# One transpose for both key blocks' factors in a sliding-window attention, with the softmax's small steps done for four heads together

## The chip, the cores and the metric

The kernel runs on one core of a Trainium2 chip. The metric is device time in microseconds (us) from launch to end. Lower is better. A core has five engines that run side by side, each with an instruction queue of its own that it works through in order: TensorE (PE in the rows; its weight loads are listed as PEld), VectorE (DVE), ScalarE (ACT), GpSimd (POOL) and SyncE (SP, here only issuing transfers). Matrix products land in PSUM, everything else lives in SBUF.

## The reference, cut to what matters

Two decoder layers run for a prompt of 1024 tokens and for 8 sample tokens. Layer 0 mixes tokens with gated linear attention, layer 1 with sliding-window attention (window 128, 16 query heads in 4 groups, one learned sink per head), and each is followed by a squared-ReLU MLP. The change lies wholly in the prompt's window attention:

```python
def sink_probs(scores, mask, sinks):
    s = jnp.where(mask, scores, -jnp.inf)
    sk = sinks.astype(jnp.float32).reshape(SWA_KV_HEADS, SWA_GROUP)[:, :, None, None]
    m = jnp.maximum(jnp.max(s, axis=-1, keepdims=True), sk)
    p = jnp.exp(s - m)
    return p / (jnp.sum(p, axis=-1, keepdims=True) + jnp.exp(sk - m))

def swa_attend_prompt(q, k, v, sinks):
    ...
    kk, vv = with_prev(k), with_prev(v)      # keys of the block before, then of the own block
    scores = jnp.einsum('bnqkgd,bnskd->bnkgqs', qb, kk).astype(jnp.float32) * (SWA_HEAD_DIM ** -0.5)
    i = jnp.arange(SWA_BLOCK)[:, None]
    j = jnp.arange(2 * SWA_BLOCK)[None, :]
    diff = SWA_BLOCK + i - j
    mask = (diff >= 0) & (diff <= SWA_WINDOW) & (key_pos >= 0)
    p = sink_probs(scores, mask[None, :, None, None], sinks)
    o = jnp.einsum('bnkgqs,bnskd->bnqkgd', p.astype(vv.dtype), vv)
```

For a query at place i of its block of 128, the mask leaves the keys j >= i of the block before and the keys j <= i of its own block. The two triangles meet only on the diagonal.

## The kernel before

The prompt is cut into two groups of 512 tokens, A (which also carries the 8 sample tokens) and B. Every weight product is a job of `lin` (L280): weights are fetched, split on ScalarE and VectorE into a rounded part and a remainder (L204, L205), and three products per tile are summed (L224, L226, L228). These jobs are the foreground.

Everything else, the attention too, is a generator in a queue `bg`. After each job `tick` (L171) hands out credit, and the front generator runs on until its `yield`s have used the credit up; `need` (L180) runs a generator to its end before a job that depends on it. So A's attention is strewn over B's first MLP, and B's attention over A's second MLP. A scheduler then decides each engine's own order, so that on ScalarE and VectorE it is not simply the order of the text.

`swa_attention` (L943) works on 16 units per group, one for each of 4 key heads and 4 blocks of 128 queries; a unit holds 4 query heads, as 2 x 2 tiles (m and i). Its steps are:
- `queries` (L969): the unit's queries are split into rounded part and remainder, two casts on ScalarE (L976, L977) and two subtractions on VectorE (L978, L979).
- `softmax` (L981): twice (for m = 0, 1) four products give scores in PSUM (L990); VectorE adds the mask and takes the maximum (L996), does small steps on 128x2 numbers (L1000 to L1002, L1007, L1008), ScalarE takes exponentials (L1004, L1006), and VectorE scales the factors in place (L1010).
- `turn` (L1013): for each of the two key blocks, four 128x128 transposes on TensorE (L1019) into a PSUM tile `ppt`, then `split` (L297) into `ph` on ScalarE (L298) and `pl` on VectorE (L299).
- `values` (L1025): four products with the values (L1030, L1031), then a few copies and sums into the output.

The first unit of each key head in A has no block before it and only one key block; the other 28 of the 32 units have two. In step i of the loop (L1042) the text has `turn` of unit i-2 and `softmax` of unit i-1, then a `yield PACE`, then `values` of unit i-2 and `queries` of unit i, then a `yield PACE`. Each stretch between two yields is called a half-step below.

The factors stand in tiles of tag `pb`, 4 buffers (`PB`); the value job's `vT`, `ko` and `srow` take the same tag. GpSimd does little in these stretches: it issues some transfers, and in the rotary step of the jobs before, it multiplies (L879) while VectorE multiplies and adds (L880, L881).

Of the kernel before, what the change touches and what calls it, by code (L numbers as in the profile page):

```python
# [12 lines left out]
F32 = mybir.dt.float32  # L13
# [7 lines left out]
P = 128  # L21
# [14 lines left out]
PB = 4  # L36
# [32 lines left out]
def tile_hybrid_gla_swa_decoder(  # L69
# [779 lines left out]
    def swa_qkv(S, sp, g, box, needs):  # L849
# [41 lines left out]
        def vjob(m):  # L891
            cell = {}

            def pre_v():
                cell["v"] = sp.tile([P, NMAX], F32, tag="pb", name="vT", bufs=PB)

# [36 lines left out]
    def swa_cache_out(sp, g):  # L933
# [4 lines left out]
        ko = sp.tile([P, 256], F32, tag="pb", name="ko", bufs=PB)  # L938
# [4 lines left out]
    def swa_attention(S, sp, g):  # L943
# [25 lines left out]
        def queries(u):  # L969
# [8 lines left out]
            nc.vector.tensor_tensor(out=qs[dn, 0], in0=q[up], in1=r(qs[up, 0]), op=ALU.subtract)  # L978
            nc.vector.tensor_tensor(out=qs[up, 1], in0=q[dn], in1=r(qs[dn, 1]), op=ALU.subtract)  # L979

        def softmax(u):  # L981
            kh, kl = keys[u.j]
            k0, n = u.k0, u.n
            u.p = []
            for m in range(2):
# [6 lines left out]
                pb = sp.tile([P, 2, 256], F32, tag="pb", name="pb", bufs=PB)  # L992
                st = sp.tile([P, 8], F32, tag="st", name="st", bufs=4)
                mx = sp.tile([P, 2], F32, tag="mx", name="mx", bufs=4)
                for i in range(2):
                    nc.vector.tensor_tensor_reduce(out=pb[:, i, k0:], in0=ps[:, i, k0:], in1=S.mask[:, k0:],  # L996
                                                   scale=1.0, scalar=-3e38, op0=ALU.add, op1=ALU.max,
                                                   accum_out=mx[:, i:i + 1])
                sk = S.sink[:, 4 * u.j + 2 * m:4 * u.j + 2 * m + 2]
                nc.vector.tensor_tensor(out=mx, in0=mx, in1=sk, op=ALU.max)  # L1000
                nc.vector.tensor_tensor(out=st[:, 0:2], in0=sk, in1=mx, op=ALU.subtract)
                nc.vector.tensor_scalar_mul(mx, mx, -1.0)  # L1002
# [3 lines left out]
                nc.scalar.activation(out=st[:, 0:2], in_=st[:, 0:2], func=AF.Exp)  # L1006
                nc.vector.tensor_tensor(out=st[:, 4:6], in0=st[:, 0:2], in1=st[:, 2:4], op=ALU.add)  # L1007
                nc.vector.reciprocal(out=st[:, 4:6], in_=st[:, 4:6])  # L1008
# [438 lines left out]
```

## Time and profile before

| | us |
|---|---|
| median of 3 runs | 2279.63 |
| the runs | 2278.18 to 2283.04 |
| the profiled execution | 2278.29 |
| its span, first to last instruction | 2276.5 |
| TensorE busy in the span | 2248.2 |
| VectorE busy | 1477.4 |
| ScalarE busy | 1233.3 |
| GpSimd busy | 83.1 |
| granted clock of TensorE, mean share of full speed | 0.998 |

The profile follows one execution. Busy time of an engine is the union of its instructions; TensorE's instructions overlap, so an instruction's own duration is longer than the distance to the next one. "Releaser" is what ended a wait.

### The profile page before, as it was taken

The numbers are of one execution on the slowest core, as the hardware profiler recorded it, in microseconds if no ns is written. First come the engines' busy times: TensorE is split into PE (matmuls) and PEld (weight loads), VectorE is DVE, ScalarE is ACT, GpSimd is POOL, SyncE is SP. The second block draws the span as 40 slices with busy tenths as digits, with TensorE's granted clock in tenths as the row PEclk, the third lists the DMA queues.
The fourth block names the chain that finished last, engine by engine and source line by source line (L and its number), as shares of the span: only waits on it lengthen the run. The fifth ranks groups of instructions, "written<-read, shape, count | busy, mean of one in ns | idle before, by whom it ended". The sixth has DMA issues, their size and how long they took to land.

```text
span 2276.5 us, 39219 instructions
## 1 busy us (share of the span) xinstructions
PE 2248.2 (99%) x14600; PEld 2041.6 (90%) x14600; DVE 1477.4 (65%) x3203; ACT 1233.3 (54%) x2608; POOL 83.1 (4%) x123
## 2 busy tenths in 40 slices
PE   7999999999999999999999999999999999999998
PEld 7998889889999998998888989989999899888886
DVE  6587666676644457566887487758888478544445
ACT  6656644466434446545776456636767456443433
POOL 3010000100000000020000000010000000000000
PEclk9999999999999999999999999999999999999999
DMA  6443322345333335333222354433222354533322
GB/s 169 130 131 99 102 79 74 111 144 163 90 93 89 93 94 171 97 111 93 79 86 73 98 168 126 135 107 86 75 75 80 93 158 130 163 117 97 102 82 81
DMA packets 389216, 247.26 MB, mean 109 GB/s; under 512 B 17848, under 2 KB 368152, under 8 KB 388224
## 3 DMA queue, kind: packets, MB, share of 16 engines
q1 hardware_dynamic: 360768, 196.85, 30.1%
q10 hardware_dynamic: 24000, 25.58, 3.8%
q0 software_dynamic: 4256, 22.31, 3.0%
q8 instruction: 115, 1.88, 0.3%
q14 instruction: 77, 0.63, 0.1%
HBM read 221.19 MB, written 24.25 MB: 108 GB/s over the span
## 4 chain that ended last, share of the span: by engine, by line
PE 54%; DVE 1%; issue 0%; ACT 0%; DMA 0%; DVEq 0%; ACTq 0%
PE psl L224 14%; PE psl L228 14%; PE psl L226 14%; PE psd L1269 2%; PE psd L1271 2%; PE psd L1270 2%; PE psc L990 1%; PE ppt L1019 1%; PE po L1030 1%; PE po L1031 1%; DVE xtail L1313 0%; PE pfin L1178 0%; DVE yf L1298 0%; DMA kc<-in_cache_swa_k_dram 0%; PE pxt L1224 0%
## 5 line engine op out<-in xcount | busy, mean ns | idle before, releaser
L224 PE MATMUL psl<-xh,wh 128*128 128x512 f32 (+2 forms) x2784 | 891.0, 320 | 0.5 <-ACT sr L532 0.3
L228 PE MATMUL psl<-xh,wl 128*128 128x512 f32 (+2 forms) x2784 | 886.3, 319 | 1.1 <-DVE wl L205 0.9
L226 PE MATMUL psl<-xl,wh 128*128 128x512 f32 (+2 forms) x2784 | 886.2, 318 | 0.2
L204 ACT CAST wh<-wst 128x512 fp32r<-128x512 f32 x656 | 405.9, 620 | 596.4 <-PE psl L226 475.7
L205 DVE TENSOR_TENSOR wl<-wst,wh 128x512 fp32r<-128x512 f32 x656 | 457.9, 700 | 301.2 <-ACT wh L204 281.5
L228 PEld LDWEIGHTS psl<-xh,wl 128*128 128x128 f32 x2784 | 523.3, 188 | 38.8 <-DVE wl L205 1.6
L224 PEld LDWEIGHTS psl<-xh,wh 128*128 128x128 f32 x2784 | 524.3, 188 | 37.1 <-ACT sr L532 0.6
L226 PEld LDWEIGHTS psl<-xl,wh 128*128 128x128 f32 x2784 | 524.1, 188 | 36.7 <-DVE xl L299 0.9
L224 PE MATMUL psl<-hh,wh 128*128 128x256 f32 (+2 forms) x1280 | 390.8, 305 | 0.0
L226 PE MATMUL psl<-hl,wh 128*128 128x256 f32 (+2 forms) x1280 | 390.7, 305 | 0.0
L228 PE MATMUL psl<-hh,wl 128*128 128x256 f32 (+2 forms) x1280 | 390.3, 305 | 0.0
L224 PEld LDWEIGHTS psl<-hh,wh 128*128 128x128 f32 x1280 | 240.9, 188 | 11.2 <-ACT hh L298 0.5
L226 PEld LDWEIGHTS psl<-hl,wh 128*128 128x128 f32 x1280 | 240.7, 188 | 11.0
L228 PEld LDWEIGHTS psl<-hh,wl 128*128 128x128 f32 x1280 | 240.8, 188 | 10.7
L299 DVE TENSOR_TENSOR hl<-rl,hh 128x256 fp32r<-128x256 f32 (+1 forms) x192 | 98.7, 514 | 166.9 <-ACT hh L298 166.3
L814 DVE TENSOR_TENSOR yf<-yf,psl 128x256 f32<-128x256 f32 (+2 forms) x280 | 132.8, 474 | 82.8 <-PE psl L228 80.7
L801 ACT ACTIVATE rl<-psl 128x256 f32<-128x256 f32 (+1 forms) x192 | 87.3, 454 | 94.9 <-PE psl L228 83.5
L1269 PE MATMUL psd<-wls,hh 128*128 128x512 f32 x256 | 101.5, 397 | 0.0
L1271 PE MATMUL psd<-whs,hh 128*128 128x512 f32 x256 | 100.6, 394 | 0.0
L1270 PE MATMUL psd<-wls,hl 128*128 128x512 f32 x256 | 100.5, 393 | 0.0
L802 ACT ACTIVATE rl<-rl 128x256 f32<-128x256 f32 (+1 forms) x192 | 94.5, 492 | 4.5
L298 ACT CAST hh<-rl 128x256 fp32r<-128x256 f32 (+1 forms) x192 | 92.3, 481 | 4.7 <-ACT rl L802 0.7
(332 smaller groups left out, 2365.2 us busy)
## 6 DMA issues: line engine op xcount, KB each, us to landing
wst<-in_ffn_w_up_dram SPq DMA_DIRECT2D x256, 256.0 KB
wst<-in_ffn_w_down_dram SPq DMA_DIRECT2D x256, 256.0 KB
wst<-in_gla_w_in_dram SPq DMA_DIRECT2D x96, 256.0 KB
wst<-in_swa_w_qkv_dram SPq DMA_DIRECT2D x48, 256.0 KB
wst<-in_gla_w_out_dram SPq DMA_DIRECT2D x32, 256.0 KB
wst<-in_swa_w_out_dram SPq DMA_DIRECT2D x32, 256.0 KB
nx<-xs ACTq DMA_DIRECT2D x24, 260.0 KB
xs<-y POOLq DMA_DIRECT2D x2, 2080.0 KB, 8.1
```

What stands on the lines that cost most here:

```text
L204: nc.scalar.copy(out=wh[:, :, :m], in_=st[:, :, :m])
L205: nc.vector.tensor_tensor(out=wl[:, :, :m], in0=st[:, :, :m], in1=r(wh[:, :, :m]), op=ALU.subtract)
L224: nc.tensor.matmul(o, lhsT=wh[:, k % 4, :m], rhs=xh[:, k, c0:c0 + n], start=(k == 0), stop=False)
L226: nc.tensor.matmul(o, lhsT=wh[:, k % 4, :m], rhs=xl[:, k, c0:c0 + n], start=False, stop=False)
L228: nc.tensor.matmul(o, lhsT=wl[:, k % 4, :m], rhs=xh[:, k, c0:c0 + n], start=False, stop=(k == kt - 1))
L298: nc.scalar.copy(out=h, in_=src)
L299: nc.vector.tensor_tensor(out=l, in0=src, in1=r(h), op=ALU.subtract)
L802: nc.scalar.activation(out=rl, in_=rl, func=AF.Square)
L814: nc.vector.tensor_tensor(out=o, in0=o, in1=ps, op=ALU.add)
L1269: nc.tensor.matmul(ps, lhsT=h[:, tok], rhs=wh, start=(k == 0), stop=False)
L1270: nc.tensor.matmul(ps, lhsT=l[:, tok], rhs=wh, start=False, stop=False)
L1271: nc.tensor.matmul(ps, lhsT=h[:, tok], rhs=wl, start=False, stop=(k == HB - 1))
```

## The change

`turn` transposes once instead of twice. For units with two key blocks, GpSimd adds the unscaled factors of the block before (`a`) onto those of the own block (`b_`), and then keeps of `a` only its diagonal (a product with the identity). The scaling by the reciprocal sum moves from VectorE to ScalarE and follows these two. Four transposes bring the summed factors into one PSUM tile; a copy under the mask `late` (j > i) takes the upper triangle into `a`, whose diagonal is there already, and a subtraction leaves the rest in `b_`. Both are then split as before, now from SBUF.

The small softmax steps are done once on 128x4 numbers instead of twice on 128x2. The two subtractions in `queries` move from VectorE to GpSimd. The factors of a unit now share one tile (2 buffers of 128x1024 instead of 4 of 128x520). The loop is reordered: `softmax` of unit i-1 and `queries` of unit i, yield, `values` of unit i-3 and `turn` of unit i-2, yield; so the transposes come three half-steps behind the scores instead of two, and the value products two behind the transposes instead of one. There are 36 yields either way. `late` is made once, from `cmask`, when the layer is set up.

```diff
-PB = 4
+PB = 2
@@ swa_setup
+        S.late = sp.tile([P, P], F32, name="late")
+        nc.gpsimd.dma_start(out=S.late, in_=cmask)
+        nc.vector.tensor_scalar(out=S.late, in0=S.late, scalar1=-1.0, scalar2=1.0, op0=ALU.mult, op1=ALU.add)
@@ queries
-            nc.vector.tensor_tensor(out=qs[dn, 0], in0=q[up], in1=r(qs[up, 0]), op=ALU.subtract)
-            nc.vector.tensor_tensor(out=qs[up, 1], in0=q[dn], in1=r(qs[dn, 1]), op=ALU.subtract)
+            nc.gpsimd.tensor_tensor(out=qs[dn, 0], in0=q[up], in1=r(qs[up, 0]), op=ALU.subtract)
+            nc.gpsimd.tensor_tensor(out=qs[up, 1], in0=q[dn], in1=r(qs[dn, 1]), op=ALU.subtract)
@@ softmax
-            u.p = []
+            pb4 = sp.tile([P, D], F32, tag="pb", name="pb", bufs=PB).rearrange("p (i m k) -> p i m k", i=2, m=2)
+            u.p = pb4
+            st = sp.tile([P, 16], F32, tag="st", name="st", bufs=4)
+            mx = sp.tile([P, 4], F32, tag="mx", name="mx", bufs=4)
             for m in range(2):
                 ps = aux([P, 2, 256], "psc")
...
-                sk = S.sink[:, 4 * u.j + 2 * m:4 * u.j + 2 * m + 2]
...
+            sk = S.sink[:, 4 * u.j:4 * u.j + 4]
+            nc.vector.tensor_tensor(out=mx, in0=mx, in1=sk, op=ALU.max)
+            nc.vector.tensor_tensor(out=st[:, 0:4], in0=sk, in1=mx, op=ALU.subtract)
+            nc.vector.tensor_scalar_mul(mx, mx, -1.0)
+            for m in range(2):
                 for i in range(2):
-                    nc.scalar.activation(out=pb[:, i, k0:], in_=pb[:, i, k0:], func=AF.Exp, bias=mx[:, i:i + 1],
-                                         accum_out=st[:, 2 + i:3 + i])
...
+                    h = 2 * m + i
+                    nc.scalar.activation(out=pb4[:, i, m, k0:], in_=pb4[:, i, m, k0:], func=AF.Exp,
+                                         bias=mx[:, h:h + 1], accum_out=st[:, 4 + h:5 + h])
+            nc.scalar.activation(out=st[:, 0:4], in_=st[:, 0:4], func=AF.Exp)
+            nc.vector.tensor_tensor(out=st[:, 8:12], in0=st[:, 0:4], in1=st[:, 4:8], op=ALU.add)
+            nc.vector.reciprocal(out=st[:, 8:12], in_=st[:, 8:12])
+            if u.first:
+                scale(u, st)
+                return
+            a, b_ = (pb4[:, :, :, c:c + P] for c in (0, P))
+            nc.gpsimd.tensor_tensor(out=b_, in0=b_, in1=a, op=ALU.add)
+            nc.gpsimd.tensor_tensor(out=a, in0=a, in1=ident.unsqueeze(1).unsqueeze(1).to_broadcast([P, 2, 2, P]),
+                                    op=ALU.mult)
+            scale(u, st)
+
+        def scale(u, st):
+            for m in range(2):
                 for i in range(2):
-                    nc.vector.tensor_scalar_mul(pb[:, i, k0:], pb[:, i, k0:], st[:, 4 + i:5 + i])
+                    pb = u.p[:, i, m, u.k0:]
+                    nc.scalar.activation(out=pb, in_=pb, func=AF.Identity, scale=st[:, 8 + 2 * m + i:9 + 2 * m + i])
@@ turn
-            for kk in ((1,) if u.first else (0, 1)):
-                pt = aux([P, 2, 2, P], "ppt")
...
+            pt = aux([P, 2, 2, P], "ppt")
+            for i in range(2):
+                for m in range(2):
+                    nc.tensor.transpose(pt[:, i, m, :], u.p[:, i, m, P:], ident)
...
+            late = S.late.bitcast(mybir.dt.uint32).unsqueeze(1).unsqueeze(1).to_broadcast([P, 2, 2, P])
+            a, b_ = (u.p[:, :, :, c:c + P] for c in (0, P))
+            nc.vector.copy_predicated(out=a, mask=late, data=pt)
+            nc.vector.tensor_tensor(out=b_, in0=pt, in1=a, op=ALU.subtract)
+            for kk, t in enumerate((a, b_)):
+                split(*halves(kk), t)
@@ the loop
-        for i in range(nu + 2):
...
+        for i in range(nu + 3):
             if 1 <= i <= nu:
                 softmax(units[i - 1])
-            yield PACE
-            if i >= 2:
-                values(units[i - 2])
             if i < nu:
                 if units[i].n == 0:
                     prep_k(units[i].j)
                 queries(units[i])
-            yield PACE
+            if i > 0:
+                yield PACE
+            if i >= 3:
+                values(units[i - 3])
+            if 2 <= i < nu + 2:
+                if units[i - 2].n == 0:
+                    prep_v(units[i - 2].j)
+                turn(units[i - 2])
+            if i < nu + 2:
+                yield PACE
```

## Rows read from the trace of the kernel before

**Rows 1.** The page: busy engines, then the chain that ended last, by line.
```profile
PE 2248.2 (99%) x14600; PEld 2041.6 (90%) x14600; DVE 1477.4 (65%) x3203; ACT 1233.3 (54%) x2608; POOL 83.1 (4%) x123
PE psl L224 14%; PE psl L228 14%; PE psl L226 14%; PE psd L1269 2%; PE psd L1271 2%; PE psd L1270 2%; PE psc L990 1%; PE ppt L1019 1%; PE po L1030 1%; PE po L1031 1%; DVE xtail L1313 0%; PE pfin L1178 0%; DVE yf L1298 0%; DMA kc<-in_cache_swa_k_dram 0%; PE pxt L1224 0%
```
**Rows 2.** TensorE's waits in 1046:1246 (A) and 1550:1783 (B): total, times, longest.
```profile
PE ppt L1019 <- DVE pb L1010: 0.5, 1, 0.5
...
PE psc L990 <- DVE kl L958: 0.3, 1, 0.3
```
**Rows 3.** Busy us by stretch, A then B: PE, PEld, DVE, ACT, POOL; clock.
```profile
1080.00:1240.00 160.00, 159.54 (x794) 133.56 (x793) 136.64 (x451) 112.18 (x294) 3.65 (x6) 1.00 0.28 81
1575.00:1745.00 170.00, 170.00 (x1388) 167.89 (x1387) 145.23 (x476) 119.83 (x332) 1.12 (x2) 1.00 0.28 79
```
**Rows 4.** Chain in order of time (start, us), then timeline of weight loads.
```profile
1603.95 0.87 PE ppt L1019 x8
...
1210.67 0.59 PEld L1019 LDWEIGHTS ppt<-ident,pb 128*128 128x128 f32 x4
...
1223.47 1.02 PEld L1019 LDWEIGHTS ppt<-ident,pb 128*128 128x128 f32 x8
```
**Rows 5.** Line L1019: duration ns min/median/max, first and last start.
```profile
L1019 PE MATMUL ppt<-ident,pb x240: 270/272/328, 1058.5 to 1772.4; 128*128 128x128 f32 x120
```
**Rows 6.** VectorE's groups in 1575:1745 (count | busy us, mean ns | idle); last row: by line.
```profile
L205 DVE TENSOR_TENSOR wl<-wst,wh 128x512 fp32r<-128x512 f32 x48 | 32.9, 687 | 4.8 <-ACT wh L204 3.6
L299 DVE TENSOR_TENSOR pl<-ppt,ph 128x512 fp32r<-128x512 f32 x24 | 15.9, 685 | 0.5
L1010 DVE TENSOR_SCALAR pb<-pb,st 128x256 f32<-128x256 f32 x48 | 14.7, 348 | 0.5
L299 DVE TENSOR_TENSOR hl<-rl,hh 128x256 fp32r<-128x256 f32 (+1 forms) x25 | 10.6, 425 | 10.4 <-ACT hh L298 10.4
L979 DVE TENSOR_TENSOR qs<-q,qs 64x256 fp32r<-64x256 f32 x12 | 5.1, 421 | 0.4
L1007 DVE TENSOR_TENSOR st<-st 128x2 f32<-128x2 f32 x24 | 3.8, 157 | 1.7 <-ACT pb L1004 1.3
...
L656 DVE COPY_PREDICATED att_sb<-cm,patt x8: 729/745/756, 101.3 to 397.5; 128x512 f32<-128x512 uint32 x8
```
**Rows 7.** ScalarE's groups in the same stretch, then single instructions from the timeline.
```profile
L802 ACT ACTIVATE rl<-rl 128x264 f32<-128x264 f32 (+1 forms) x24 | 10.1, 422 | 0.4
...
1606.24 0.40 ACT L977 CAST qs<-q 64x256 fp32r<-64x256 f32 x1
...
1609.16 0.49 ACT L1004 ACTIVATE pb<-pb,mx 128x256 f32<-128x256 f32 x1
```
**Rows 8.** Timeline of GpSimd and VectorE where GpSimd multiplies (start, us, idle before).
```profile
1515.26 1.28 POOL L879 TENSOR_TENSOR qsw<-qsw,sin 128x512 f32<-128x512 f32 x1 [4.14 <-DMA qsw<-q]
1515.77 1.32 DVE L205 TENSOR_TENSOR wl<-wst,wh 128x512 fp32r<-128x512 f32 x1 [0.71 <-ACT wh L204]
...
1547.77 1.29 POOL L879 TENSOR_TENSOR qsw<-qsw,sin 128x512 f32<-128x512 f32 x1 [4.16 <-DMA qsw<-q]
1548.30 0.43 DVE L814 TENSOR_TENSOR yf<-yf,psl 128x264 f32<-128x264 f32 x1 [1.02 <-PE psl L228]
```
**Rows 9.** VectorE's idle time ahead of L881 (20 instructions): releaser, us, times.
```profile
  POOL qsw L879: 1.1, 2
```
**Rows 10.** Timelines of one unit's scores and scaling; then the shortest stretch in A.
```profile
1605.49 0.28 PE L990 MATMUL psc<-kl,qs 128*128 128x256 f32 x1
1611.26 0.62 DVE L1010 TENSOR_SCALAR pb<-pb,st 128x256 f32<-128x256 f32 x2
...
1155.13 0.39 PE L1030 MATMUL po<-ph,vv 128*128 128x512 f32 x1
...
1168.60 0.37 PEld L1019 LDWEIGHTS ppt<-ident,pb 128*128 128x128 f32 x2
1169.66 0.68 PEld L1019 LDWEIGHTS ppt<-ident,pb 128*128 128x128 f32 x6 [0.69 <-DVE pb L1010]
```

More of the change, by code (lines that the diff above doesn't have):

```diff
@@ L894, in pre_v @@
             def pre_v():
-                cell["v"] = sp.tile([P, NMAX], F32, tag="pb", name="vT", bufs=PB)
+                cell["v"] = sp.tile([P, D], F32, tag="pb", name="vT", bufs=PB)
             def ev(ps, c0, n):
@@ L937, in swa_cache_out @@
             nc.tensor.transpose(pt[:, m, :], g.kr[:, m, P + 384:P + 512], ident)
-        ko = sp.tile([P, 256], F32, tag="pb", name="ko", bufs=PB)
+        ko = sp.tile([P, D], F32, tag="pb", name="ko", bufs=PB)[:, :256]
         nc.vector.tensor_copy(out=ko, in_=pt.rearrange("p m d -> p (m d)"))
@@ L991, in softmax @@
                                          start=(kx is kh), stop=(kx is kl))
-                pb = sp.tile([P, 2, 256], F32, tag="pb", name="pb", bufs=PB)
-                st = sp.tile([P, 8], F32, tag="st", name="st", bufs=4)
-                mx = sp.tile([P, 2], F32, tag="mx", name="mx", bufs=4)
                 for i in range(2):
-                    nc.vector.tensor_tensor_reduce(out=pb[:, i, k0:], in0=ps[:, i, k0:], in1=S.mask[:, k0:],
+                    nc.vector.tensor_tensor_reduce(out=pb4[:, i, m, k0:], in0=ps[:, i, k0:], in1=S.mask[:, k0:],
@@ L1006, in softmax @@
-                nc.scalar.activation(out=st[:, 0:2], in_=st[:, 0:2], func=AF.Exp)
-                nc.vector.tensor_tensor(out=st[:, 4:6], in0=st[:, 0:2], in1=st[:, 2:4], op=ALU.add)
-                nc.vector.reciprocal(out=st[:, 4:6], in_=st[:, 4:6])
+                                                   accum_out=mx[:, 2 * m + i:2 * m + i + 1])
+            sk = S.sink[:, 4 * u.j:4 * u.j + 4]
+            nc.vector.tensor_tensor(out=mx, in0=mx, in1=sk, op=ALU.max)
+            nc.vector.tensor_tensor(out=st[:, 0:4], in0=sk, in1=mx, op=ALU.subtract)
@@ L1009, in softmax @@
                 for i in range(2):
-                    nc.vector.tensor_scalar_mul(pb[:, i, k0:], pb[:, i, k0:], st[:, 4 + i:5 + i])
-                u.p.append(pb)
+                    pb = u.p[:, i, m, u.k0:]
+                    nc.scalar.activation(out=pb, in_=pb, func=AF.Identity, scale=st[:, 8 + 2 * m + i:9 + 2 * m + i])
         def turn(u):
             u.pt = {}
-            for kk in ((1,) if u.first else (0, 1)):
-                pt = aux([P, 2, 2, P], "ppt")
-                for i in range(2):
-                    for m in range(2):
-                        nc.tensor.transpose(pt[:, i, m, :], u.p[m][:, i, kk * P:(kk + 1) * P], ident)
-                ph = sp.tile([P, 2, 2, P], F32R, tag="ph", name="ph", bufs=PT)
-                pl = sp.tile([P, 2, 2, P], F32R, tag="pl", name="pl", bufs=PT)
-                split(ph, pl, pt)
-                u.pt[kk] = ph, pl
+            pt = aux([P, 2, 2, P], "ppt")
@@ new lines, in turn, with halves @@
+            for i in range(2):
+                for m in range(2):
+                    nc.tensor.transpose(pt[:, i, m, :], u.p[:, i, m, P:], ident)
+            def halves(kk):
+                u.pt[kk] = (sp.tile([P, 2, 2, P], F32R, tag="ph", name="ph", bufs=PT),
+                            sp.tile([P, 2, 2, P], F32R, tag="pl", name="pl", bufs=PT))
+                return u.pt[kk]
+            if u.first:
+                split(*halves(1), pt)
+                return
+            late = S.late.bitcast(mybir.dt.uint32).unsqueeze(1).unsqueeze(1).to_broadcast([P, 2, 2, P])
@@ L1080, in swa_samples @@
                 nc.tensor.transpose(pt[:, m, :], t[:, m, :], ident)
-            row = sp.tile([NS, 256], F32, tag="pb", name="srow", bufs=PB)
+            row = sp.tile([P, D], F32, tag="pb", name="srow", bufs=PB)[:NS, :256]
             nc.vector.tensor_copy(out=row, in_=pt.rearrange("p m d -> p (m d)"))
```

8 lines of the change are left out of this document (removed).

## The prediction

> **What bounds the kernel now.** I read the page's busy times first, then the chain that ended last, then the waits of the two stretches in which the attention runs, and last the prices of single instructions. TensorE is busy 2248.2 of 2276.5 us, and the chain that ends last is almost wholly TensorE's own products [rows 1]. The attention's steps lie between foreground products: over A's whole attention TensorE waits 0.5 us, over B's 0.3 us [rows 2]. At the full clock and with no gap [rows 3], whatever leaves TensorE's queue leaves the span, and whatever the other engines do costs nothing until TensorE has to wait for it. So two questions decide: how much time do the removed transposes take in TensorE's queue, and have the other engines room for what replaces them?
>
> **What TensorE loses.** There are 240 transposes now [rows 5]: 28 units with 8 and 4 first units with 4. After the change there are 128. 112 go, four in each of 28 units; products with scores and values stay. A transpose is listed with 272 ns [rows 5], but that is its own length, and they overlap. Their price is the distance from one to the next: eight in a row hold the chain for 0.87 us, which is 0.109 each; a group of four loads spans 0.59 and one of eight 1.02 us, so four more take 0.43 us [rows 4]. The removal is worth 28 x 0.435 = **12.2 us**.
> The Trainium skill's page "TensorE: Matmul & The Clock Gate", in its part on the PE-mode transpose, gives about 275 ns for a 128x128 transpose within a kernel. The length in the trace agrees, and by that figure as a price the removal would be an estimated 31 us. The chain does not pay it, since it pays distances, so I don't use it.
>
> **What VectorE loses and gains, per full unit** [rows 6]. It loses four scalings (4 x 0.348 = 1.39 us), one of two rounds of five small operations (row of L1007, 5 x 0.157 = 0.79), two query subtractions (0.84) and the two split subtractions out of PSUM (1.37): 4.39. It gains a predicated copy of 128x512 out of PSUM, for which the row of L656 has the same shape (0.745), the subtraction of `a` from PSUM (0.685) and two split subtractions from SBUF (as L205, 1.37): 2.80. Net: 1.59 us less. B's stretch of 170 us holds 12 units (48 scalings, four per unit), and VectorE idles 24.8 us in it, 2.06 per unit; in A it is busy for the same share, 0.854 [rows 3], and 16 units in the 200 us of A's attention [rows 2] make 12.5 us a unit, so it idles 1.8. After the change it would idle 3.65 (B) and 3.4 (A), if nothing held it up.
>
> **What ScalarE gains.** Four scalings of 128x256 within SBUF. L802 is the same kind at 0.42 us, an exponential at 0.49 is the upper bound [rows 7]: 1.7 to 2.0 us, less one small exponential. I take 1.6 net. ScalarE idles 4.18 per unit in B and 3.7 in A [rows 3], so 2.6 and 2.1 us are left.
>
> **What GpSimd gains.** Per full unit one addition and one product of 128x512 and two subtractions of 64x256. A product of 128x512 takes 1.28 us there [rows 8]. The smaller ones aren't in the trace: bounds are half of that, 0.64, by their elements per partition, and all of it, 1.28, if a fixed part prevails; I take 0.64, as VectorE's own rows fall from 0.685 to 0.42 with that size [rows 6]. Sum 3.8 (up to 5.1) us of a unit's 12.5 to 14.2. GpSimd has room; its queue holds little else there (3.65 and 1.12 us busy [rows 3]), transfers included.
>
> **Whether GpSimd holds VectorE up.** The rows show that it does: while L879 multiplies on GpSimd, L205, which reads two tiles in SBUF, takes 1.32 instead of 0.69 us and ends after GpSimd does; L814, with one operand in PSUM, keeps its 0.43 [rows 8]. The Trainium skill's page "SBUF — State Buffer", section "Who interferes with whom", says that a VectorE instruction with two SBUF inputs and a GpSimd instruction that reads SBUF shut each other out for a whole instruction; both rows agree with it. How often does that strike? In B's stretch L205 is busy 32.9 us, the like subtraction for `hl` 10.6 [rows 6], and the new splits add 12 x 1.37 = 16.4; with the attention's output remainders some 65 of 170 us, 0.38 of the time. At that share a unit's 3.8 us of GpSimd cost VectorE 1.5 us, and it idles about 2.0 us, as it does now. So I price this at nothing on TensorE.
>
> **Longer chain, earlier start.** From the end of the scores to the end of the scaling takes 6.1 us now (1605.77 to 1611.88 [rows 10]). GpSimd's two steps add 2.6, with a wait for VectorE at each up to 4.0, and the slower scaling 0.6: about 9.3 to 10.7 us. In return, the transposes stand three half-steps behind the scores. The new place of the scores is that of the value products of two units before; the shortest such distance in A is 1155.13 to 1168.60, 13.5 us, 3 us more than needed. In the same place of today's kernel the transposes came too early and waited 0.69 us [rows 10]; that wait goes.
>
> **Buffers, setup, end.** A factor tile comes free only after the splits, one half-step before its next use; both stand in VectorE's queue in that order, so this delays nothing that TensorE needs. `late` costs one transfer and one operation on 128x128 long before its use: nothing. At a phase's end the last transposes and value products may follow each other directly, with the predicated copy and a subtraction more between them (1.43 us): 0 to 2.9 us for both, against 0.8 us of waits that may go. I take zero for the sum of these, from -0.8 to +2.9.
>
> **The sum.** The profiled execution took 2278.29 us (span 2276.5), 1.3 below the median of the runs. 2278.29 - 12.2 = 2266.1 for such an execution, and 2279.63 - 12.2 = **2267.4** for the median.
>
> **Rivals.**
> *The shut-out eats the gain.* If every microsecond of GpSimd stops VectorE, it lacks 3.8 - 3.65 = 0.15 us per unit in B and 0.4 in A, and TensorE follows: 16 x 0.15 + 12 x 0.4 = 7 us, 2275. With GpSimd at 5.1 it would be 16 x 1.45 + 12 x 1.7 = 44 us, 2311, the far end. For it: the measured shut-out. Against: much of what VectorE does has an operand in PSUM. I take 2275 to 2281 as its likely form. Chance 0.12.
> *ScalarE stands in line behind GpSimd (slower).* The four scalings wait for GpSimd's two steps. If they stand at the head of ScalarE's queue, weight casts and evictions queue behind them, and TensorE waits for those. It decides from 2.1 (A) to 2.6 us (B) per unit. At 2.6 it costs 12 x 0.5 = 6 us, 2273; at 4.0, 16 x 1.4 + 12 x 1.9 = 45 us, **2312**. Against: queues aren't in the order of the text; the casts of the next unit's queries (L977), which the text has after the softmax, come at 1606.24, ahead of its exponentials at 1609.16 [rows 7]. And where VectorE has a step behind GpSimd today, L881, it idled only 1.1 us over 20 of them [rows 9]. Chance 0.11.
> *It does not do what it says:* the removed time comes back as waits for late transposes or late casts elsewhere, 2277 to 2281, no change. Against: TensorE's waits in both phases are 0.8 us in all. Chance 0.07.
>
> **How the numbers follow.** Forecast 0.70, with a range of its own from 2264 (spread of the runs, waits gone) to 2272 (phase ends, a little lateness). A measurement of this kernel tells 0.2%, 4.6 us, from no change, so faster means below 2275.1. Faster: 0.70 and a third of the first rival, 0.74. Same: the rest of that rival's likely form and most of the third, 0.14. Slower: 0.12, the queue rival and the far end of the first. The range 2264 to 2279 holds the forecast, two thirds of the first rival and most of the third, about 0.81.
>
> **What would show it.** Right: 128 transposes, the chain's share of L1019 halved, TensorE's busy time lower by 12 us, waits in the attention under 2 us per phase, GpSimd near 4 us per unit, VectorE's share in these stretches near or under 0.85. Wrong: TensorE's waits before L1019 released by ScalarE (chain too long), before foreground products released by L204 (ScalarE in line) or by L205 with lengths near 2 us (shut-out).

## The result, and the profile after

The changed kernel takes 2327.89 us in the median of 5 runs (2325.12 to 2329.22), the kernel before 2279.63 in as many runs beside it (2278.18 to 2283.04): a ratio of 1.0212, with a 95% interval from 1.0200 to 1.0223. It is 48 us slower, where 12 us faster was forecast, and it lies outside the predicted range. The profiled execution took 2327.73 us, with a span of 2326.0.

The page of the changed kernel, busy engines and then the chain that ended last, by engine and by line:

```profile
PE 2258.1 (97%) x14488; PEld 2041.2 (88%) x14488; DVE 1478.3 (64%) x2908; ACT 1273.5 (55%) x2704; POOL 220.2 (9%) x244
PE 75%; DVE 8%; ACT 6%; issue 4%; DMA 3%; POOL 3%; ACTq 0%; SPq 0%; DVEq 0%; POOLq 0%
PE psl L224 21%; PE psl L226 21%; PE psl L228 21%; PE psd L1302 2%; PE psd L1304 2%; PE psd L1303 2%; ACT pb L1030 2%; POOL pb L1022 1%; POOL pb L1021 1%; DVE wl L205 1%; DVE pb L1000 1%; DVE pl L299 1%; ACT wh L204 1%; DMA wst<-in_gla_w_in_dram 1%; PE pP L678 1%
```

The transposes did go: 14488 products instead of 14600 [rows 1]. Yet the chain now carries ScalarE's scaling (L1030) and GpSimd's two steps (L1022, L1021), 4% together. TensorE is busy 10 us more in spite of fewer products, for which a lower clock, shown below, accounts in part; the rest of the added span is waiting. TensorE's waits from 1040 to 1840 us, both attentions (total, times, longest):

```profile
PE psl L224 <- ACT rl L801: 16.7, 7, 4.8
PE psl L224 <- DVE yf L814: 7.9, 7, 1.9
PE psl L228 <- DVE wl L205: 4.1, 3, 1.4
PE po L1061 <- DVE pl L299: 3.7, 5, 1.7
...
PE ppt L1037 <- ACT pb L1030: 0.5, 1, 0.5
```

Before, the two rows of [rows 2] were all there was. The transposes themselves wait 0.5 us, as they did. Of the 39.8 us of waits in this stretch some 29 stand ahead of foreground products (L224, L228), for the evictions and remainders of the MLP that B's or A's attention is strewn over, and 9.2 ahead of the attention's value products (L1060, L1061). The same stretches as in [rows 3], then one of 20 us (us, busy us of PE, PEld, DVE, ACT, POOL, granted clock, then two columns on transfers):

```profile
1080.00:1240.00 160.00, 154.09 (x724) 126.93 (x723) 125.48 (x312) 120.99 (x317) 46.77 (x46) 0.98 0.26 77
1575.00:1745.00 170.00, 148.95 (x1119) 142.59 (x1118) 126.90 (x308) 115.93 (x316) 51.58 (x45) 0.95 0.22 63
1660.00:1680.00 20.00, 15.09 (x99) 14.46 (x98) 14.86 (x36) 13.16 (x34) 5.40 (x5) 0.83 0.21 60
```

In B's 170 us TensorE got through 1119 products where it had done 1388. No engine is full: VectorE idles 43 us, ScalarE 54, GpSimd 118. And behind some of the gaps the clock is lower.

One gap shows how it comes about. The chain of waits through 1655 to 1668 us, cut (start, us, what):

```profile
1656.35 0.61 DVE mx L1004
1656.96 3.13 issue
1660.09 1.29 POOL pb L1021
...
1661.45 1.60 POOL pb L1022
...
1663.08 1.70 ACT pb L1030 x4
1664.78 0.29 ACT hh L298
...
1665.48 0.36 ACT ot L1066
...
1665.87 0.62 ACT ph L298
1666.49 0.30 ACT rl L801
```

The 3.13 us of "issue" hold VectorE's next small steps and then the exponentials, which ScalarE ends at 1659.96. GpSimd then adds and multiplies until 1663.05. ScalarE has a relu and a weight cast in between and then comes to the four scalings, for which it stands 2.03 us. Behind them in its queue are a cast of the MLP (`hh`), two copies and a cast of the attention, and only then, at 1666.40, the relu `rl` that frees the PSUM tile of the next chunk. TensorE, which ran dry at 1662.0, starts again at 1666.83. Its own timeline there (start, us, idle before):

```profile
1659.80 0.28 PE L226 MATMUL psl<-hl,wh 128*128 128x256 f32 x1
1659.91 0.28 PE L228 MATMUL psl<-hh,wl 128*128 128x256 f32 x1
...
1661.72 0.28 PE L228 MATMUL psl<-hh,wl 128*128 128x264 f32 x1
1666.83 0.58 PE L224 MATMUL psl<-hh,wh 128*128 128x256 f32 x1 [4.83 <-ACT rl L801]
...
1667.86 0.41 PE L226 MATMUL psl<-hl,wh 128*128 128x256 f32 x1
1668.07 0.41 PE L228 MATMUL psl<-hh,wl 128*128 128x256 f32 x1
...
1672.36 0.28 PE L228 MATMUL psl<-hh,wl 128*128 128x264 f32 x1
1672.48 0.28 PE L224 MATMUL psl<-hh,wh 128*128 128x264 f32 x1
```

Ahead of the gap equal products (128x256) follow each other at 0.11 to 0.12 us, after it at 0.21: TensorE, having stood for 4.83 us, goes on at the lower of its two levels (1.2 instead of 2.4 GHz), until 1672.36, and the stretch's mean of 0.83 is a mix of the two. So this gap is paid twice. Not every one is, and length alone does not tell which: behind a gap of 2.64 us that ends at 1176.78 the lower level stands, behind one of 3.13 us that ends at 1800.11 it doesn't:

```profile
1178.00:1180.00 2.00, 2.00 (x8) 1.81 (x7) 2.00 (x9) 1.96 (x5) 0.73 (x1) 0.50 0.17 49
1800.00:1802.00 2.00, 1.67 (x12) 1.47 (x12) 1.97 (x5) 2.00 (x7) 0.00 (x0) 1.00 0.00 0
```

Over the whole span the mean granted clock fell from 0.998 to 0.993, by estimate some 0.005 x 2326 = 12 us. ScalarE's waits from 1040 to 1840:

```profile
ACT pb L1030 <- POOL pb L1022: 53.8, 27, 3.0
ACT st L1012 <- DVE st L1005: 44.1, 24, 3.8
```

The first is new: there are 27 such waits for 28 full units, 2.0 us each. The second, the sinks' exponential waiting for VectorE's step behind the maximum, was 23.1 us over 21 before.

### The profile page after: what moved, and what is told of

The parts are those of the page before. It is cut to its first block, busy times and chain, and to the rows that moved or that the text cites. A ratio compares the mean times of both kernels' runs of the same rounds, so it can differ in the third digit from the quotient of the medians.

```text
span 2326.0 us, 39012 instructions
## 1 busy us (share of the span) xinstructions
PE 2258.1 (97%) x14488; PEld 2041.2 (88%) x14488; DVE 1478.3 (64%) x2908; ACT 1273.5 (55%) x2704; POOL 220.2 (9%) x244
## 4 chain that ended last, share of the span: by engine, by line
PE 75%; DVE 8%; ACT 6%; issue 4%; DMA 3%; POOL 3%; ACTq 0%; SPq 0%; DVEq 0%; POOLq 0%
PE psl L224 21%; PE psl L226 21%; PE psl L228 21%; PE psd L1302 2%; PE psd L1304 2%; PE psd L1303 2%; ACT pb L1030 2%; POOL pb L1022 1%; POOL pb L1021 1%; DVE wl L205 1%; DVE pb L1000 1%; DVE pl L299 1%; ACT wh L204 1%; DMA wst<-in_gla_w_in_dram 1%; PE pP L678 1%
## 5 line engine op out<-in xcount | busy, mean ns | idle before, releaser
L224 PE MATMUL psl<-xh,wh 128*128 128x512 f32 (+2 forms) x2784 | 892.9, 321 | 5.0 <-ACT rl L801 3.6
L228 PE MATMUL psl<-xh,wl 128*128 128x512 f32 (+2 forms) x2784 | 886.7, 319 | 5.2 <-DVE wl L205 5.0
L204 ACT CAST wh<-wst 128x512 fp32r<-128x512 f32 x656 | 404.1, 619 | 544.4 <-PE psl L226 423.5
L205 DVE TENSOR_TENSOR wl<-wst,wh 128x512 fp32r<-128x512 f32 x656 | 480.7, 736 | 292.5 <-ACT wh L204 273.9
L228 PEld LDWEIGHTS psl<-xh,wl 128*128 128x128 f32 x2784 | 523.4, 188 | 43.8 <-DVE wl L205 6.9
L224 PEld LDWEIGHTS psl<-xh,wh 128*128 128x128 f32 x2784 | 524.4, 188 | 42.5 <-ACT rl L801 4.2
L224 PE MATMUL psl<-hh,wh 128*128 128x256 f32 (+2 forms) x1280 | 398.0, 311 | 21.4 <-ACT rl L801 13.1
L228 PE MATMUL psl<-hh,wl 128*128 128x256 f32 (+2 forms) x1280 | 393.7, 308 | 0.0
L224 PEld LDWEIGHTS psl<-hh,wh 128*128 128x128 f32 x1280 | 244.3, 191 | 35.2 <-ACT rl L801 14.6
L228 PEld LDWEIGHTS psl<-hh,wl 128*128 128x128 f32 x1280 | 244.1, 191 | 11.0
L801 ACT ACTIVATE rl<-psl 128x256 f32<-128x256 f32 (+1 forms) x192 | 87.0, 453 | 91.1 <-PE psl L228 79.1
```

What stands on the lines that cost most here:

```text
L204: nc.scalar.copy(out=wh[:, :, :m], in_=st[:, :, :m])
L205: nc.vector.tensor_tensor(out=wl[:, :, :m], in0=st[:, :, :m], in1=r(wh[:, :, :m]), op=ALU.subtract)
L224: nc.tensor.matmul(o, lhsT=wh[:, k % 4, :m], rhs=xh[:, k, c0:c0 + n], start=(k == 0), stop=False)
L228: nc.tensor.matmul(o, lhsT=wl[:, k % 4, :m], rhs=xh[:, k, c0:c0 + n], start=False, stop=(k == kt - 1))
```

## The experiments

The theory after the comparison: ScalarE stands at the head of its queue behind GpSimd, and evictions and casts stand behind it. Rivals: GpSimd shuts VectorE out; the longer chain or the new loop makes the transposes late; ScalarE is short of time for the added scalings. Each row was run beside the kernel before, and the ratio is to that; "on" says which kernel the edit is made to.

| run | on | edit | median us | ratio (95%) |
|---|---|---|---|---|
| e1_scale_first | after | scaling ahead of GpSimd's steps | 2298.15 | 1.0084 (1.0069 to 1.0099) |
| e2_scale_later | after | scaling a half-step later in the text | 2321.56 | 1.0184 (1.0167 to 1.0201) |
| e3_queries_back | after | queries' subtractions on VectorE | 2324.33 | 1.0200 (1.0185 to 1.0215) |
| e4_scale_vector | after | scaling on VectorE | 2330.37 | 1.0228 (1.0212 to 1.0243) |
| e13_rl_two | after | room for two chunks in `rl` | 2327.37 | 1.0208 (1.0191 to 1.0225) |
| e5_two_heads | e1 | small softmax steps twice, for two heads | 2307.35 | 1.0120 (1.0105 to 1.0136) |
| e16_pieces | e1 | GpSimd's two steps in eight | 2293.64 | 1.0057 (1.0042 to 1.0072) |
| e8_no_blocks | e1 | GpSimd's two steps left out | 2278.09 | 0.9993 (0.9984 to 1.0003) |
| e7_blocks_vector | e1 | GpSimd's two steps on VectorE | 2283.62 | 1.0020 (1.0011 to 1.0029) |
| e10_no_gpsimd | e7 | and the queries' subtractions | 2277.04 | 0.9991 (0.9981 to 1.0000) |
| e14_no_gpsimd_rl_two | e10 | and room for two chunks in `rl` | 2278.31 | 0.9998 (0.9989 to 1.0008) |
| e9_loop_only | before | new loop | 2279.69 | 1.0002 (0.9993 to 1.0012) |
| e12_scale_scalar | e9 | scaling on ScalarE | 2282.70 | 1.0019 (1.0009 to 1.0029) |
| e17_four_heads | before | small steps for four heads at once | 2281.70 | 1.0011 (1.0001 to 1.0021) |
| e18_two_turns | before | loop, scaling, four heads, queries on GpSimd | 2289.65 | 1.0046 (1.0029 to 1.0063) |
| e19_two_turns_idle | e18 | idle products on GpSimd | 2289.46 | 1.0046 (1.0031 to 1.0061) |
| e11_idle_gpsimd | before | eight idle products of 128x128 | 2279.25 | 1.0004 (0.9995 to 1.0014) |
| e15_long_idle | before | four idle products of 128x256 | 2281.21 | 1.0009 (1.0000 to 1.0018) |

### Who stands behind GpSimd: e1, e2, e4

e1 keeps every instruction and moves one call.

```diff
+            scale(u, st)
             if u.first:
-                scale(u, st)
                 return
...
                                     op=ALU.mult)
-            scale(u, st)
```

> The changed kernel with one swap: ScalarE scales the four factors before GpSimd adds the blocks and keeps the diagonal, not after. The same instructions, the same chain from scores to transposes; only ScalarE no longer has an instruction in its queue that waits for GpSimd. Theory 'ScalarE stands in line behind GpSimd' (53.8 us of waits ahead of the scaling in 27 of 28 units, weight casts and the MLP's evictions behind them): the waits go and with them most of 60 us, 2265 to 2285 us, TensorE idle in both attention phases under 10 us together. Rival 'GpSimd shuts VectorE out': GpSimd does the same work, so 2310 us or more. Rival 'the new order of the loop and the softmax for four heads': also 2310 or more.

It gives back 1.0212 - 1.0084 = 0.0128, 29 us of the 48. More was expected (2265 to 2285 us), so a second cause had to be sought. TensorE's waits in e1, same stretch:

```profile
PE psl L224 <- ACT rl L801: 6.2, 4, 2.7
PE psl L224 <- DVE yf L814: 5.0, 7, 1.6
PE po L1059 <- DVE vv L970: 2.3, 1, 2.3
PE ppt L1036 <- POOL pb L1021: 2.0, 2, 1.3
```

ScalarE has no wait for GpSimd any more, and TensorE's wait for `rl` fell from 16.7 to 6.2 us. With the work unchanged, this much is the scaling's place in the queue and nothing else.

e2 issues the same scalings one half-step later in the text:

```diff
-            scale(u, st)
+            u.st = st
...
+            if 1 <= i <= nu and not units[i - 1].first:
+                scale(units[i - 1], units[i - 1].st)
             if i >= 3:
                 values(units[i - 3])
```

> The changed kernel with the four scalings of the full units issued one half-step later (behind the next yield, ahead of the value products), still after GpSimd. Theory 'ScalarE in line': the same dependence, but GpSimd has long been done when ScalarE comes to it; waits for GpSimd ahead of the scaling under 10 us in all instead of 53.8, 2268 to 2290 us. A remainder over the swap would be the shorter time left until the transposes. Rival 'shut-out' or 'loop order': 2310 or more.

It gives back 6 us, little more than the intervals, where 38 or more were expected. ScalarE still waits for GpSimd, 50.9 us in 27 waits after 53.8 in 27: the scheduler's order, not the text's, is the queue, and it kept the scalings where they wait.

e4 lets VectorE stand there in ScalarE's stead:

```diff
-                    nc.scalar.activation(out=pb, in_=pb, func=AF.Identity, scale=st[:, 8 + 2 * m + i:9 + 2 * m + i])
+                    nc.vector.tensor_scalar_mul(pb, pb, st[:, 8 + 2 * m + i:9 + 2 * m + i])
```

> The changed kernel with the four scalings back on VectorE, still after GpSimd. Theory 'an engine that feeds TensorE stands in line behind GpSimd': now VectorE stands there for the same 2 us a unit, with the weight remainders and the MLP's sums behind it, and does 1.4 us more work: 2300 to 2340 us. If it is ScalarE's part alone that matters (evictions and the casts of hh), 2270 to 2285. Rival 'shut-out': 2320 or more, with longer L205.

No better: VectorE's wait (first row, 1040 to 1790) is shorter, and TensorE's waits in the same stretch come from VectorE's evictions now.

```profile
DVE pb L1030 <- POOL pb L1022: 29.3, 23, 2.0
PE psl L224 <- DVE yf L814: 13.9, 8, 2.9
PE psl L224 <- ACT rl L801: 7.3, 3, 2.6
PE psl L228 <- DVE wl L205: 6.8, 4, 2.6
```

So it is not ScalarE's load. Either engine has evictions of the foreground in its queue, and either costs TensorE time when it stands behind GpSimd.

### Through which buffer the wait arrives: e13, e14

`rl` has one buffer; I took that for the place where ScalarE's wait reaches TensorE.

```diff
-                    rl = hp.tile([P, 512], F32, tag="rl", name="rl", bufs=1)[:, :n]
+                    rl = rl_t[0][:, c0:c0 + n]
```

> The changed kernel with room for two chunks of the MLP's relu: `rl`, which had one buffer, is a tile of two halves, so that a chunk's relu need not wait until the chunk before it is cast and its remainder taken. If ScalarE's wait behind GpSimd reaches TensorE through that one buffer, the waits of TensorE for `rl` (16.7 us) shrink and the time falls to 2300 to 2315 us. If it reaches TensorE because ScalarE itself comes late to everything (relu, casts, scaling in one queue), nothing shrinks: 2322 us or more.

It changes nothing, and its waits (1040 to 1790) say why:

```profile
PE psl L224 <- ACT wh L204: 7.4, 5, 2.2
PE psl L224 <- DVE yf L816: 7.4, 6, 2.3
PE psl L224 <- ACT rl L803: 4.9, 2, 3.2
```

The wait for `rl` is smaller (13.5 in that stretch of the changed kernel) and a wait for weight casts stands in its place. That theory fell: ScalarE as a whole is late, and whatever it owes TensorE next is what TensorE waits for. The same edit to e10, where nobody stands behind GpSimd, brings nothing either.

> e10_no_gpsimd (the change with nothing on GpSimd, scaling ahead, 2277.0 us) with the same second half of `rl`. In e10 TensorE still waits 3.2 us for `rl`. If one buffer is what is left, 2270 to 2274 us; if ScalarE and VectorE are what is left, 2276 to 2278 us.

### What GpSimd's two steps cost besides: e8, e7, e16

e8 leaves the two steps out of e1; e7 puts them on VectorE; e16 cuts each into four of 128 columns. The edit of e16:

```diff
-            nc.gpsimd.tensor_tensor(out=b_, in0=b_, in1=a, op=ALU.add)
-            nc.gpsimd.tensor_tensor(out=a, in0=a, in1=ident.unsqueeze(1).unsqueeze(1).to_broadcast([P, 2, 2, P]),
-                                    op=ALU.mult)
+            for m in range(2):
+                for i in range(2):
+                    x, y = a[:, i, m, :], b_[:, i, m, :]
+                    nc.gpsimd.tensor_tensor(out=y, in0=y, in1=x, op=ALU.add)
+                    nc.gpsimd.tensor_tensor(out=x, in0=x, in1=ident, op=ALU.mult)
```

> The kernel that scales first, with GpSimd's addition and diagonal left out: the block before is not summed in, so what it computes is another sum. GpSimd keeps the queries' subtractions. Theory 'GpSimd shuts VectorE out' (2.6 us of two-operand work per unit beside VectorE, and its place in the chain) for the rest of 31 us: 2268 to 2280. If the rest is due to the softmax for four heads, the loop or the longer turn: 2292 to 2300.

> The kernel that scales first, with the addition and the diagonal on VectorE: no shut-out from these two, but 1.4 us more of VectorE's own time per unit. If VectorE's lateness by shut-out costs more than that work: 2280 to 2292. If not: 2298 to 2310.

> e1_scale_first (2298.2 us) with GpSimd's addition and diagonal product in eight instructions of 128 columns in place of two of 512. The same work at the same place, in steps of some 0.4 to 0.6 us. If the length of one step is what costs, near e8's 2278 to 2288 us; if the work's place in the chain is what costs (the transposes wait for GpSimd), 2298 us or more.

Without the steps e1 falls by 0.0091, 21 us. On VectorE, which has more to do already, they cost 6 us instead of 21. In pieces they cost 15. TensorE's waits in e16 (1040 to 1790):

```profile
PE ppt L1038 <- POOL pb L1024: 5.2, 4, 2.3
PE psl L224 <- DVE yf L814: 4.6, 6, 1.3
PE psl L224 <- ACT rl L801: 4.4, 2, 2.2
```

In e8 the last two are 2.9 and 3.6 us and the first is absent. Short steps therefore mend three tenths, and most of the cost is left when GpSimd's single step is short. The cut also made GpSimd's work longer, though: its two steps take 2.65 us of a unit in e1 and 4.24 in e16 (eight of 0.53), so e16 alone does not part the length of a step from the length of the chain.

### Length or place: e11, e15, e18, e19

GpSimd multiplies something that nobody reads: in e11 and e15 in the kernel before, in e19 in e18, which has all of the change but the single transpose and GpSimd's steps for it. The edit of e19:

```diff
+            if not u.first:
+                for h in range(4):
+                    nc.gpsimd.tensor_tensor(out=S.idle, in0=S.mask.rearrange("p (a b) -> p a b", a=2),
+                                            in1=st[:, 8:10].unsqueeze(2).to_broadcast([P, 2, P]), op=ALU.mult)
```

> The kernel before, computing all that it did, with eight idle products of 128x128 on GpSimd per full unit (as many elements as the addition and the diagonal), which start when the unit's reciprocals are there and which nobody waits for. Theory 'shut-out': VectorE's instructions with two operands in SBUF, and its scalings, are held; VectorE comes to over 0.9 of the attention's stretches and TensorE waits for it: 2287 to 2310 us. Rival 'only the queue behind GpSimd counts': no engine has a new wait in its queue, so 2277 to 2282.

> The kernel before with four idle products of 128x256 on GpSimd in every full unit, whose result nobody reads. GpSimd then works as long in a unit as it does in the changed kernel, in steps near 0.9 us where e11 had 0.58. If GpSimd costs by shutting VectorE out for the length of one step, 2283 us or more; if it costs only where another engine waits for its result, 2279 to 2280 us.

> The change without its core: four heads at once, scaling on ScalarE, queries' subtractions on GpSimd and the new loop, but both key blocks transposed as in the kernel before, so no long step on GpSimd. The parts run alone cost 0 (loop), 3 (scaling) and 3 us (four heads), and the queries on GpSimd up to 7 by e7 against e10: 2283 to 2292 us if such costs add. Above 2295 us if, with less idle time left to ScalarE and VectorE, they cost more together.

> e18_two_turns with four idle products of 128x256 on GpSimd in every full unit, right behind the scaling, whose result nobody reads: GpSimd's load of e1_scale_first, in a kernel whose other engines are as late and as busy as in the changed one, but without a place in the chain. If e1's 20 us over e8 come from GpSimd's place (the transposes wait for it), within 4 us of e18. If they come from VectorE being held up, which costs nothing in the kernel before but may here, 10 us or more above e18.

B's stretch in e15, then in e18, then in e19 (columns as above):

```profile
1575.00:1745.00 170.00, 169.99 (x1385) 167.62 (x1384) 155.60 (x476) 118.81 (x332) 40.08 (x51) 1.00 0.27 78
```
```profile
1575.00:1745.00 170.00, 164.77 (x1312) 160.46 (x1312) 117.99 (x321) 128.16 (x350) 19.49 (x24) 0.99 0.25 74
```
```profile
1575.00:1745.00 170.00, 164.29 (x1319) 159.77 (x1318) 120.77 (x321) 128.51 (x351) 53.98 (x72) 1.00 0.26 75
```

e19 keeps GpSimd as busy as the changed kernel does, 54 against 52 us of 170, and costs nothing beside e18. In e15 VectorE is busy 155.60 us instead of the 145.23 of [rows 3], since it is held up, and the kernel loses 2 us, about its interval. These idle steps take 0.78 us (e15) and 0.72 (e19), half of what the real ones take (1.30 and 1.35 in e1), and VectorE has more idle time beside them in e19 than in e1 (49 against 32 us of 170), so e19 alone doesn't speak for the real ones; e16 has these in pieces and loses 15 us. Together they speak for GpSimd's place in the chain and against its load. No run has long steps that nobody waits for, so that the hold of a long step on VectorE has a share in the 21 us isn't ruled out.

No single wait carries the 21 us: TensorE's waits from 1040 to 1840 add up to 19.2 us in e1 and 7.9 in e8, spread over relus, sums, remainders and the transposes, and it is busy 8.4 us longer (2247.2 and 2238.8) at a mean clock of 0.996 instead of 0.998. In e16 5.2 us are the transposes' own wait. Which step passes the lateness on is open.

### The parts without GpSimd's steps: e9, e12, e17, e3, e5, e10

The loop alone, then ScalarE's scaling on top of it, and the small steps for four heads alone (the edits are those of the change; e12's scaling is shown):

```diff
-                    nc.vector.tensor_scalar_mul(pb[:, i, k0:], pb[:, i, k0:], st[:, 4 + i:5 + i])
+                    nc.scalar.activation(out=pb[:, i, k0:], in_=pb[:, i, k0:], func=AF.Identity,
+                                         scale=st[:, 4 + i:5 + i])
```

> The kernel before with nothing but the new order of the loop: the softmax and the next queries share a half-step, value products and transposes the other, transposes three half-steps behind the scores, value products two behind the transposes. All eight transposes, VectorE's scaling and the two-head steps stay. If the order is harmless: 2276 to 2282 us. If the order itself makes some of the 31 us that were left after ScalarE's scaling was put ahead of GpSimd (2298 against 2279 with 12.2 us less for TensorE): 2285 to 2310, with TensorE waiting before the value products and the MLP's products.

> The kernel before with the new loop order and the factors' scaling on ScalarE instead of VectorE; nothing else, GpSimd as before. It prices ScalarE's 1.6 us more per unit and its place in line behind VectorE's reciprocals alone. If that makes the 11 us that stayed when GpSimd's two steps were left out (2278 against 2267): 2285 to 2292 us, with TensorE waiting for ScalarE's evictions (L801). If ScalarE has room, as I had it: 2276 to 2282, or a little less.

> The kernel before with the softmax's steps for four heads at once alone: transposes, scaling, queries' subtractions and loop as before. If the loss comes from what stands in line behind GpSimd, and the four heads' chain of exponentials, sum and reciprocal stalls nobody by itself, 2278 to 2281 us. If ScalarE's and VectorE's waits on each other inside that chain (25 us of VectorE behind the exponentials in e8, against 2.8 us in the kernel before) reach TensorE, 2285 us or more.

They cost 0, 4 and 2.5 us. e18, with the queries' subtractions on GpSimd as well, costs 10.5, so some 4 us go to those or to the parts together. A row of e18 in B's stretch, and one of its eleven maxima beside GpSimd's subtraction, show what the subtractions do:

```profile
L1000 DVE TENSOR_TENSOR mx<-mx,sink 128x4 f32<-128x4 f32 x11 | 7.7, 697 | 0.0
...
1589.41 0.94 POOL L978 TENSOR_TENSOR qs<-q,qs 64x256 fp32r<-64x256 f32 x1 [14.53 <-ACT qs L976]
...
1589.67 0.70 DVE L1000 TENSOR_TENSOR mx<-mx,sink 128x4 f32<-128x4 f32 x1
```

This maximum of 128x4 numbers takes 0.157 us in e10 (and that of 128x2 numbers 0.154 in the kernel before); here, with GpSimd subtracting, 0.697, and it ends with GpSimd's instruction (1590.35 and 1590.37). It is the first of the small steps, and the exponentials wait for it. The Trainium skill's page "SBUF — State Buffer", section "Who interferes with whom", has a VectorE instruction with two SBUF inputs and a GpSimd instruction that reads SBUF contend for an exclusive lock; this row agrees. Moving the subtractions back is worth 3 us in the changed kernel, about as much as the intervals, and 7 from e7 to e10:

```diff
-            nc.gpsimd.tensor_tensor(out=qs[dn, 0], in0=q[up], in1=r(qs[up, 0]), op=ALU.subtract)
+            nc.vector.tensor_tensor(out=qs[dn, 0], in0=q[up], in1=r(qs[up, 0]), op=ALU.subtract)
```

> The changed kernel with the two subtractions of the queries back on VectorE; GpSimd keeps the addition and the diagonal. GpSimd's work per unit falls from 4.6 to 2.9 us, VectorE's own grows by 0.84. Theory 'ScalarE in line': the wait behind GpSimd stays, 2315 to 2335 us. Rival 'shut-out': two fifths of GpSimd's blocking go, and with them a like share of 60 us, 2300 to 2310.

> The changed kernel with the scaling first and all that GpSimd did in the attention back on VectorE: addition, diagonal and the queries' subtractions. VectorE does 2.2 us more per unit than in the kernel that scales first with GpSimd (2298), and nothing shuts it out. Theory 'shut-out': the queries' share of it goes too, so no slower than with the queries on GpSimd (2284): 2276 to 2284 us. Rival 'VectorE is simply full': 0.84 us more per unit at 0.86 busy: 2288 to 2300.

e10 is the fastest variant, and no faster than the kernel before by what can be measured: B's stretch there, where VectorE and ScalarE both are fuller than in [rows 3] and TensorE got through 1335 products (four transposes fewer per unit, 48, explain most of the 53 less):

```profile
1575.00:1745.00 170.00, 165.95 (x1335) 161.93 (x1334) 151.97 (x414) 135.42 (x366) 1.12 (x2) 1.00 0.27 77
```

e5 undoes the four heads inside e1 and costs 8 us, where a gain was expected if the four heads were to blame:

> The kernel that scales first, with the small softmax steps, exponentials and scalings done for two heads at a time, as before. Theory 'four heads at once': ScalarE waits 43.7 us for the step L1005 (23.1 us before the change) since its first exponential needs the maxima of all four heads; with two heads at a time that falls to about 23 us and the time to 2280 to 2290. Otherwise 2295 to 2305, VectorE having 0.8 us more per unit.

The wait that it was to shorten stayed (ScalarE behind L1005, 40.5 us after 43.7), so that theory fell. In the kernel before, four heads at once lost 2.5 us; here they gain 8. Why is open; twice as many small steps that GpSimd can hold up would be a reason, but no run shows it.

### The sum of the loss

From the ratios: parts beside the single transpose +10.5 us (e18); the removed transposes -12 (e18 to e8, 0.0053); GpSimd's steps in the chain, with nobody but the transposes behind them, +21 (e8 to e1); ScalarE behind them +29 (e1 to the changed kernel). Together +48. They must add up, since each kernel is the next one's start; what is shown is the price of each difference. The scheduler orders each kernel anew, and no run parts an edit from the new order that comes with it.

## Why the prediction was wrong, step by step

Forecast and result lie 60 us apart. 29 of them are the queue rival, ScalarE behind GpSimd, which the prediction let begin only at 2.1 us per unit; 21 are GpSimd's two steps in the chain, which "Longer chain, earlier start" put at nothing; 10.5 are the parts beside the transposes (loop, scaling, four heads, the queries' subtractions), which the sum put at nothing on TensorE because the other engines had idle time. With the scaling first and all of GpSimd's share back on VectorE the change is still no faster than the kernel before (e10).

**What TensorE loses** held. Between e18 and e8, which differ in the second set of transposes and in what splits the result, lie 12.1 us by the ratios, whose intervals are 4 and 2 us to either side, and TensorE's busy time is 2251.8 and 2238.8 us. 12.2 were forecast, from distances. By the length that the Trainium skill's page "TensorE: Matmul & The Clock Gate" gives in its part on the PE-mode transpose, for bf16, the estimate was 31 us; these runs rule that out as a price here, while as a length it agrees (0.272 us).

**What ScalarE gains** had the right size and the wrong test. The four scalings take 1.70 us (1663.08 above), the wait ahead of them 2.0 us. The step that failed here is the point from which the queue rival was to decide, 2.1 to 2.6 us per unit. That was ScalarE's idle time per unit, a budget. The measured wait lies below it and, by that rule, would have cost nothing; it cost 29 us. Idle time that lies elsewhere in the unit doesn't pay for a stand of 2 us at a place where the next chunk's eviction is behind it: TensorE's foreground has three PSUM tiles (`psl`) to run ahead with, and ScalarE's stand from 1661.06 is TensorE's gap from 1662.0 on, though ScalarE idles 54 of 170 us. The rival was named, with the right place, and dismissed at 0.11 on two arguments. That the scheduler reorders queues was true (e2) and no help, as it ordered this one so that there are 27 waits for 28 units. That L881 idled 1.1 us in all behind L879 [rows 9] was a row of another step on another engine and at another place of its queue; it said nothing of where the scheduler would put this one. The sign named for this rival, foreground products released by L204, was hardly seen (0.5 us); the same engine's `rl` (L801) was what they waited for.

**The clock** was no term of the sum. At 1.00 throughout [rows 3] it seemed fixed; behind some of the gaps it is not, and by the estimate above some 12 us went there.

**What GpSimd gains** was nearly right: 3.8 (to 5.1) us per unit forecast, 4.6 measured. GpSimd's groups from 1040 to 1790:

```profile
L1022 POOL TENSOR_TENSOR pb<-pb,ident 128x512 f32<-128x512 f32 x26 | 39.6, 1525 | 2.0
L1021 POOL TENSOR_TENSOR pb<-pb 128x512 f32<-128x512 f32 x26 | 35.6, 1371 | 93.8 <-issue 66.6 <-ACT pb L1010 18.7 <-ACT st L1012 8.4
L983 POOL TENSOR_TENSOR qs<-q,qs 64x256 fp32r<-64x256 f32 x30 | 26.9, 895 | 9.7 <-ACT qs L981 7.9 <-DVE mx L1000 0.2
L982 POOL TENSOR_TENSOR qs<-q,qs 64x256 fp32r<-64x256 f32 x30 | 24.4, 812 | 210.0 <-ACT qs L980 209.7
```

**Whether GpSimd holds VectorE up.** It does, by nearly the amount reckoned: by the prediction's 1.59 us of work less per unit VectorE should be busy 44.5 us less, and it is busy 1478.3 us after 1477.4, so that by estimate the hold took 1.6 us a unit (1.5 reckoned). As capacity short idle steps cost next to nothing, as priced (e11, e15, e19). What the step missed is which instructions it meets: a maximum of 0.15 us that stands ahead of the exponentials takes 0.70. What that costs by itself no run shows; the part of e18 that its other parts leave over, some 4 us, bounds it.

**Longer chain, earlier start.** The transposes wait for the scaling 0.5 us, so the room reckoned was there and the new loop is free (e9). But the sum counted only the transposes as waiting for the chain. e1 still pays 21 us for GpSimd's two steps in it.

**Buffers, setup, end.** The factors' buffers cost nothing that a wait shows. At the end of A's attention, 1240 to 1290 us, the value products wait 5.2 us, where 2.9 was the bound for both phases; no run tried this by itself. A wait of 2.6 us for `vv` falls in the middle of A (it ends at 1176.78).

```profile
PE po L1061 <- DVE pl L299: 2.9, 3, 1.7
PE po L1060 <- ACT ph L298: 2.3, 2, 1.2
```

**The other rivals.** The shut-out as lost capacity, 2275 to 2311 us by the prediction, finds no support in e19, whose steps are half as long. That the removed time comes back as waits is refuted for e8 against e18, but it is what e10 looks like: there TensorE is busy 6.6 us less than before (2241.6 and 2248.2) and waits 7.1 us from 1040 to 1840, where it had waited 0.8.

**Chances.** 0.12 stood on slower. All of the sum rested on waits of 0.8 us in the trace of before, which is a statement on that order of queues. Every step that adds a wait across engines makes a new one.

## What to carry to other kernels

When a step moves to another engine, ask what stands in line behind the instruction that waits for it, and how far ahead the bounding engine can run without that; idle time per unit of work is no cushion for it. Put the waiting step on the queue ahead of the slow producer, as e1 does, or, which no run here tried, on an engine that owes the foreground nothing. A trace without gaps shows no price for one: here a gap of 4.83 us cost its length and then 5.5 us at half the clock, one of 3.13 us its length alone.

## What the runs showed of the hardware that I had not expected

- TensorE fell to its lower level behind a gap of 4.83 us and stayed there for 5.5 us of products: 0.12 to 0.21 us from one 128x256 product to the next, granted clock 0.83 over the 20 us around it. Behind one of 3.13 us it went on at full clock.
- GpSimd takes 0.81 and 0.90 us for a subtraction of 64x256, more than half of the 1.37 us of an addition of 128x512. The product with the identity, an operand repeated by its access pattern, takes 1.53 us.
- A VectorE instruction of 128x4 numbers took 0.70 instead of 0.15 us beside GpSimd's subtractions: the hold goes by GpSimd's instruction, not by VectorE's.
- 34 us more of GpSimd's work in 170 us, for nobody, cost no time that shows (e19 beside e18: 53.98 and 19.49 us busy).
